# An MLP whose second product is done by Strassen's scheme in one level, after the first product as a whole

## The chip, the core and the metric

The kernel runs on one core of a Trainium2 chip. A core has a matrix engine (TensorE, PE in the profile, with its weight loads listed as PEld), three engines for elementwise work (VectorE = DVE, ScalarE = ACT, GpSimd = POOL), a queue engine that issues transfers (SyncE = SP) and 16 DMA engines. On-chip memory is SBUF, with PSUM for the results of the matrix engine; DRAM lies outside the core. The metric is the device time of one execution in microseconds (us); lower is better. Columns of a tile are its elements along the free axis.

## The reference, cut to what matters

The kernel computes one layer of a streaming encoder: a mixer (latent attention beside a state-space scan) and an MLP. The change touches only the MLP, the last stage:

```python
D_MODEL, D_FF, SEQ, N_META, DEC_SEQ = 1024, 4096, 1024, 16, 32

def hybrid_layer(h, ...):
    ...                                   # attention, scan, gates
    h = h + merged @ p["w_out"]
    a = jax.nn.relu(rmsnorm(h, p["norm_mlp"]) @ p["w_mlp_up"])     # 1024 -> 4096
    h = h + (a * a) @ p["w_mlp_down"]                              # 4096 -> 1024
    return h, ...
```

In the MLP the prompt's 1024 rows and the sample's 32 rows go through together, so that a tile has NQT = 1056 columns, one for each row of h, with D_MODEL or D_FF on the partitions. Everything is f32.

## The kernel before, in words

**Numbers.** To keep f32 accuracy, each operand of a product is split in two parts of type fp32r: hi is a copy of the value in that type (ACT, line 183), lo is the value less hi (DVE or POOL, line 186). A product is three passes into one PSUM sum: hi by hi, hi by lo, lo by hi. `lin_part` issues them: for each block k of 128 contraction rows, for each of the three passes, one matmul for each chunk of columns, `CQ` being three chunks of 352. All its matmuls have one line in the profile, 269; `lin2` gives PSUM tiles of two pools in turn, named acc and pj. Every matmul has a weight load (LDWEIGHTS) of its own.

**Weights.** `Weights` holds the list of all weight units in the order of their use, and each is loaded into a tile `raw` (one DMA on SP's queue) and split into `wh` (ACT) and `wl` (in the MLP POOL), loaded two units ahead of the use and split one ahead. A unit of the first product is 8 blocks of 128 by 128 (512 KB, 1024 columns when split), one of the second is 4 blocks (256 KB, 512 columns).

**The MLP.** The first product gives D_FF = 4096 hidden rows, as 32 units `up(f)` of 128 rows: 72 matmuls of 352 columns each (8 blocks, 3 passes, 3 chunks). Each chunk is then scaled and cut at zero (DVE, line 1492, reading PSUM), squared (ACT, 1493) and split into `ah` (ACT) and `al` (DVE). Four units make a group, eight groups the whole. `down(q)` takes group q's four `ah`/`al` pairs and adds its part of the second product to the 8 accumulators `yacc[:, m]`, 128 rows of the output by 1056 columns each: 36 matmuls of 352 columns for an m, then three DVE additions (line 1510) from PSUM. So first and second product alternate by groups, and nothing of the hidden rows leaves the chip. The accumulators start as h, loaded from DRAM (`h_d`, line 1482) ahead of the MLP.

**Order and end.** The order on each engine is that in which a scheduler puts the instructions of the program; DMAs of the MLP all stand on SP's one queue. In the last group each finished m is turned by PE (transposes of 128 columns, line 1519, `out_rows`), copied by ACT (1521) and stored (1522); the 32 sample rows go by `ys`, a transpose (1541) and `yos` (1543, 1544). The last m of all is done chunk by chunk (396, 396 and 264 columns), so that the outputs of one chunk lie beside the matmuls of the next.

## Time and profile before

| what | value |
|---|---|
| time, median of 3 runs | 2076.12 us (2072.12 to 2077.6) |
| the profiled execution: its own time | 2074.39 us |
| its span, first to last instruction | 2072.6 us |
| mean granted TensorE clock, as a share of full speed | 0.997 |
| PE busy | 2024.0 us, 12944 matmuls |
| DVE, ACT, POOL busy | 1101.4, 731.0, 594.7 us |
| read from and written to DRAM | 123.95 and 44.41 MB |

The rows are all of one execution, whose time lies 1.8 us above its span. A busy time is a sum over an engine's instructions; matmuls are pipelined, so that their listed durations overlap, and how fast PE goes is read from the starts of successive matmuls or from their number in a stretch. The MLP runs from about 1326 us to the end.

### The profile page before, as it was taken

To read this page: it belongs to the slowest core of one execution; us is meant where nothing else is said; L and a number is where in the kernel's file an instruction comes from. 1 tells how busy PE (TensorE), PEld (TensorE's weight loads), DVE (VectorE), ACT (ScalarE), POOL (GpSimd) and SP (SyncE) were. 2 spreads that over 40 slices of the span, in tenths; PEclk is the share of its full clock that TensorE was granted. 3 is DMA by queue.
4 is the path that set the end of the run, shared out by engine and by line. 5 is a ranking of instruction groups with operands and counts; after the bars stand their busy time and mean duration, and the time that the engine had idled before them with its cause. 6 is when DMAs were issued, how large, how long until landed. Compare 5 with 4: busy or idle time off the path is not lost.

```text
span 2072.6 us, 33999 instructions
## 1 busy us (share of the span) xinstructions
PE 2024.0 (98%) x12944; PEld 1917.2 (93%) x12944; DVE 1101.4 (53%) x3071; ACT 731.0 (35%) x1738; POOL 594.7 (29%) x794
## 2 busy tenths in 40 slices
PE   7999999999999999999998999999999999999999
PEld 6988888899999788888887999999999999999998
DVE  5969776534666688888885544332322223222222
ACT  4213222223332567676755233321221212122222
POOL 0577776621222123121221012112221221212121
PEclk9999999999999999999999999999999999999999
DMA  5334444435443101110113534412111120212113
GB/s 144 116 111 120 138 118 143 134 120 173 133 129 117 52 11 28 17 28 17 26 35 98 195 99 132 165 31 57 36 52 51 36 67 26 61 31 57 41 41 105
DMA packets 255893, 170.57 MB, mean 82 GB/s; under 512 B 63210, under 2 KB 239169, under 8 KB 255730
## 3 DMA queue, kind: packets, MB, share of 16 engines
q1 hardware_dynamic: 255728, 168.40, 27.9%
q8 instruction: 102, 1.67, 0.3%
q14 instruction: 61, 0.50, 0.1%
q10 hardware_dynamic: 2, 0.00, 0.0%
HBM read 123.95 MB, written 44.41 MB: 81 GB/s over the span
## 4 chain that ended last, share of the span: by engine, by line
PE 84%; DVE 10%; DMA 3%; ACT 1%; issue 1%; POOL 0%; SPq 0%; ACTq 0%; DVEq 0%; POOLq 0%
PE acc L269 40%; PE pj L269 22%; PE pj L1050 3%; PE po L1283 3%; PE pj L1115 2%; PE pt L1258 1%; PE sp L678 1%; PE Sp L1201 1%; PE Sp L1193 1%; PE Sp L1194 1%; PE Sp L1196 1%; PE Sp L1195 1%; DVE clt L421 1%; PE sp L622 1%; PE pj L1160 1%
## 5 line engine op out<-in xcount | busy, mean ns | idle before, releaser
L186 POOL TENSOR_TENSOR wl<-raw,wh 128x1024 fp32r<-128x1024 f32 (+1 forms) x148 | 291.3, 1968 | 952.2 <-ACT wh L183 853.9
L183 ACT ACTIVATE wh<-raw 128x1024 fp32r<-128x1024 f32 (+2 forms) x166 | 148.6, 895 | 749.1 <-PE acc L269 351.7
L269 PE MATMUL acc<-xh,wh 128*128 128x264 f32 (+6 forms) x736 | 188.7, 337 | 1.8 <-ACT xh L183 1.8
L269 PE MATMUL acc<-xh,wl 128*128 128x264 f32 (+4 forms) x736 | 181.1, 327 | 0.0
L269 PE MATMUL acc<-xl,wh 128*128 128x264 f32 (+5 forms) x736 | 181.0, 327 | 0.0
L269 PEld LDWEIGHTS acc<-xh,wh 128*128 128x128 f32 (+1 forms) x736 | 127.2, 190 | 14.1 <-issue 7.3
L269 PEld LDWEIGHTS acc<-xl,wh 128*128 128x128 f32 (+1 forms) x736 | 129.7, 190 | 2.1 <-issue 0.7
L269 PEld LDWEIGHTS acc<-xh,wl 128*128 128x128 f32 (+1 forms) x736 | 129.6, 190 | 1.8 <-issue 0.7
L1510 DVE TENSOR_TENSOR yacc<-pj,yacc 128x352 f32<-128x352 f32 x96 | 44.5, 517 | 139.5 <-PE pj L269 139.5
L1510 DVE TENSOR_TENSOR yacc<-acc,yacc 128x352 f32<-128x352 f32 (+1 forms) x96 | 44.5, 518 | 113.0 <-PE acc L269 113.0
L186 DVE TENSOR_TENSOR al<-t,ah 128x352 fp32r<-128x352 f32 x96 | 64.7, 700 | 71.9 <-ACT ah L183 71.9
L269 PE MATMUL acc<-sh,wh 128*128 128x352 f32 x384 | 93.0, 325 | 1.5 <-ACT sh L753 1.5
L269 PE MATMUL acc<-sl,wh 128*128 128x352 f32 x384 | 93.5, 324 | 0.0
L269 PE MATMUL acc<-sh,wl 128*128 128x352 f32 x384 | 93.0, 324 | 0.0
L1492 DVE SCALAR_TENSOR_TENSOR t<-acc,rstd 128x352 f32<-128x352 f32 x48 | 23.5, 517 | 117.8 <-PE acc L269 117.8
L269 PE MATMUL acc<-ah,wl 128*128 128x352 f32 (+1 forms) x384 | 85.2, 324 | 0.0
L269 PE MATMUL pj<-al,wh 128*128 128x352 f32 x384 | 84.6, 324 | 0.0
L269 PE MATMUL pj<-ah,wh 128*128 128x352 f32 x384 | 84.3, 323 | 0.0
L269 PE MATMUL acc<-al,wh 128*128 128x352 f32 (+1 forms) x384 | 84.1, 323 | 0.0
L269 PE MATMUL acc<-ah,wh 128*128 128x352 f32 (+1 forms) x384 | 84.0, 323 | 0.0
L269 PE MATMUL pj<-ah,wl 128*128 128x352 f32 x384 | 84.0, 323 | 0.0
L269 PE MATMUL pj<-ha,wh 128*128 128x352 f32 x360 | 79.1, 324 | 0.0
(470 smaller groups left out, 5319.9 us busy)
## 6 DMA issues: line engine op xcount, KB each, us to landing
raw<-in_w_mlp_up_dram SPq DMA_DIRECT2D x32, 512.0 KB
raw<-in_w_mlp_down_dram SPq DMA_DIRECT2D x64, 256.0 KB
raw<-in_w_in_dram SPq DMA_DIRECT2D x29, 512.0 KB
ud<-gst SPq DMA_DIRECT2D x8, 536.0 KB
U<-ud SPq DMA_DIRECT2D x64, 67.0 KB
yd<-Y SPq DMA_DIRECT2D x64, 66.0 KB
yt<-yd SPq DMA_DIRECT2D x8, 528.0 KB
sd<-gw SPq DMA_DIRECT2D x8, 528.0 KB
```

The costliest lines, as they stand in the source:

```text
L183: nc.scalar.activation(hi, src, AF.Copy)
L186: lo_eng.tensor_tensor(lo, src, hi.bitcast(F32), ALU.subtract)
L269: nc.tensor.matmul(pt[:M, :n], lhsT=w[:, k, :], rhs=x(k, c0, n), start=(k == 0 and p == 0), stop=(k == kt - 1 and p == 2),)
L421: eng.tensor_tensor(t1, ar, br, ALU.mult)
L622: nc.tensor.matmul(px[64 * g2:64 * g2 + 64, KC * q:KC * q + KC], lhsT=W[:, q, g, 64 * g2:64 * g2 + 64], rhs=U[:, 2 * g + g2], start=True, ...
L678: nc.tensor.matmul(py[b][:, c], lhsT=cl[hs, q, pr, 1:9].rearrange("p a b -> p (a b)"), rhs=hb[hs, q, pr], start=False, stop=(q == 1),)
L1050: nc.tensor.matmul(ps[:R], lhsT=x[:, c, k0:k0 + R], rhs=w[:, c, :], start=(c == 0 and q == 0), stop=(c == 1 and q == 2))
L1115: nc.tensor.matmul(ps[:R, :384], lhsT=x[:, c, 128 * i:128 * i + R], rhs=w[:, c, :], start=(c == 0 and q == 0), stop=(c == 2 and q == 2))
L1160: nc.tensor.transpose(pt[:, h, z, :R], qt[:, e, h, z], ident[:R, :R])
L1283: nc.tensor.matmul(po[:, :256], lhsT=w, rhs=x, start=st["first"], stop=(last and q == len(grp) - 1))
L1492: nc.vector.scalar_tensor_tensor(t, ps, 0.0, rstd[:, c], op0=ALU.max, op1=ALU.mult)
L1510: nc.vector.tensor_tensor(yacc[:, m, c], ps, yacc[:, m, c], ALU.add)
```

## The change

The 32 units of the first product now run first, all in one go. A group's hidden rows are four blocks k of 128 by 1056; Strassen's scheme (in Winograd's form) cuts them into halves of blocks (two and two) and halves of columns (528 and 528), makes seven blocks of two by 528 out of the four quarters, four by DVE subtractions and three as they are, and each of the seven is split into hi and lo (`place0` to `place6`, 1.08 MB each: 128 partitions by 2112 values). For the groups 0 to 6 they are stored in DRAM (`bd0_0` to `bd6_6`); the seven of group 7 stay. Then the second product runs over 32 pairs: 8 groups (7 first, then 0 to 6, read back into a ring of 12 places) by 4 pairs of output tiles. For a pair POOL makes four sums of weight quarters (128 by 256 each), ACT and POOL split 1024 and 768 columns of weights, and PE does seven products of 12 matmuls (2 blocks, 3 passes, 2 chunks of 264 columns), 84 in all. DVE adds PSUM to `yacc` seven times (`gather`, 128 by 528). Products lie in PSUM tiles X (two buffers), Y and Z (one buffer each, Y also for the outputs' transposes). Before, the same work was 8 quarter products: 2 x 36 matmuls of 352 columns for two output tiles. The accumulators are loaded after the first product; the code before this stage is moved by a few lines (so 269 is 264 there) and otherwise as it was.

```diff
-    units += ups(0, range(GK))
     for q in range(NG):
-        if q + 1 < NG:
-            units += ups(q + 1, [0])
-        units += [(col(flat("w_mlp_down")[q * 512:(q + 1) * 512], m), GK, 128) for m in range(8)]
-        if q + 1 < NG:
-            units += ups(q + 1, range(1, GK))
+        units += ups(q, range(GK))
...
-        yacc = ml.tile([128, 8, NQT], F32, name="yacc")
-        for m in range(8):
-            nc.sync.dma_start(yacc[:, m], h_d[m])
-        ring = {}
...
-            for c0, n, ps in lin2(wh, wl, rh, rl, 8):
-                c = slice(c0, c0 + n)
-                t = ml.tile([128, 352], F32, tag="t", name="t", bufs=2)[:, :n]
-                nc.vector.scalar_tensor_tensor(t, ps, 0.0, rstd[:, c], op0=ALU.max, op1=ALU.mult)
-                nc.scalar.activation(t, t, AF.Square)
-                split(ah[:, c], al[:, c], t, nc.scalar, nc.vector)
-            ring[f] = (ah, al)
...
-        for f in range(GK):
-            up(f)
-        for q in range(NG):
-            if q + 1 < NG:
-                up((q + 1) * GK)
-            down(q)
-            if q + 1 < NG:
-                for f in range(1, GK):
-                    up((q + 1) * GK + f)
...
+    HN = NQT // 2
+    HS = HN // 2
+    blk_d = [dscr(f"bd{q}_", 7, (128, 4 * HN)) for q in range(NG - 1)]
...
+    place = [ml.tile([128, 2, 2, HN], F32R, name=f"place{i}") for i in range(7)]
...
+        for c0, n, ps in lin2(wh, wl, rh, rl, 8):
+            c = slice(c0, c0 + n)
+            t = mu.tile([128, 352], F32, tag="t", name="t", bufs=2)[:, :n]
+            nc.vector.scalar_tensor_tensor(t, ps, 0.0, rstd[:, c], op0=ALU.max, op1=ALU.mult)
+            nc.scalar.activation(a_[:, e % 2, c], t, AF.Square)
+        def keep(i, x):
+            split(place[i][:, 0], place[i][:, 1], x, nc.scalar, nc.vector)
+            if q < NG - 1:
+                nc.sync.dma_start(blk_d[q][i], flat_blk(place[i]))
+        V = nc.vector
+        b1, b2 = hid[0], hid.get(1)
+        lo_, hi_ = slice(0, HN), slice(HN, NQT)
+        if e == 1:
+            hid["t"] = tA = mu.tile([128, 2, HN], F32, tag="tA", name="tA")
+            keep(0, b1[:, :, lo_])
+            V.tensor_tensor(tA, b1[:, :, hi_], b1[:, :, lo_], ALU.subtract)
+            keep(1, tA)
+        if e == 3:
+            tA = hid["t"]
+            V.tensor_tensor(tA, b2[:, :, hi_], tA, ALU.subtract)
+            keep(2, tA)
+            keep(3, b2[:, :, hi_])
+            keep(4, b2[:, :, lo_])
+            V.tensor_tensor(b1[:, :, hi_], b2[:, :, hi_], b1[:, :, hi_], ALU.subtract)
+            keep(5, b1[:, :, hi_])
+            V.tensor_tensor(b1[:, :, lo_], b2[:, :, lo_], tA, ALU.subtract)
+            keep(6, b1[:, :, lo_])
...
+    order = [NG - 1] + list(range(NG - 1))
+    pairs = [(g, j) for g in range(NG) for j in range(4)]
...
+    def w_sums(n):
+        r1, r2 = raws[2 * (n % 2):2 * (n % 2) + 2]
+        T_ = nc.gpsimd.tensor_tensor
+        T_(B(r1, 2), B(r2, 0), B(r2, 1), ALU.add)
+        T_(B(r1, 3), B(r1, 2), B(r1, 0), ALU.subtract)
+        return lambda: (T_(B(r2, 2), B(r1, 0), B(r2, 0), ALU.subtract), T_(B(r2, 3), B(r1, 1), B(r1, 3), ALU.subtract))
+    def w_split(n, e):
+        (h_, l_), r = whl[2 * (n % 2) + e], raws[2 * (n % 2) + e]
+        c = slice(256 * e, 1024)
+        split(h_[:, c], l_[:, c], r[:, c], nc.scalar, nc.gpsimd)
...
+    OPS = {1: (0, 0, 0), 5: (0, 2, 1), 6: (0, 3, 2), 3: (1, 3, 3), 2: (0, 1, 4), 7: (1, 2, 5), 4: (1, 1, 6)}
+    for f in range(NG * GK):
+        up(f)
+        if f == NG * GK - 2:
...
+    rights.close()
+    banks.close()
...
+    yps = ctx.enter_context(tc.tile_pool(reuse_waits="tile", name="yps", bufs=1, space=PSUM))
+    zps = ctx.enter_context(tc.tile_pool(reuse_waits="tile", name="zps", bufs=1, space=PSUM))
+    xps = ctx.enter_context(tc.tile_pool(reuse_waits="tile", name="xps", bufs=2, space=PSUM))
+    yacc = [md.tile([128, NQT], F32, name=f"yacc{m}") for m in range(8)]
+    for m in range(2):
...
+    place += [md.tile([128, 2, 2, HN], F32R, name=f"place{i}") for i in range(7, 12)]
...
+    def blk_load(x):
+        g, i = divmod(x, 7)
+        if g < NG:
+            nc.sync.dma_start(flat_blk(place[x % 12]), blk_d[order[g]][i])
...
+    def prod(n, p, ps, first, halves=((0, 1),)):
+        g, j = pairs[n]
+        e, wb, i = OPS[p]
+        (h_, l_), x = whl[2 * (n % 2) + e], place[(7 * g + i) % 12]
+        for hs in halves:
+            for k in range(2):
+                for q, (w, u) in enumerate(((h_, 0), (h_, 1), (l_, 0))):
+                    for s in hs:
+                        nc.tensor.matmul(ps[:, s, :HS], lhsT=w[:, 256 * wb + 128 * k:256 * wb + 128 * k + 128],
+                                         rhs=x[:, u, k, HS * s:HS * s + HS],
+                                         start=(first and k == 0 and q == 0), stop=(k == 1 and q == 2), skip_group_check=True)
+        if j == 3:
+            blk_load(7 * g + i + 12)
+    def gather(n, r, c, ps, hs=None):
+        y_ = yacc[2 * pairs[n][1] + r][:, HN * c:HN * c + HN].rearrange("p (s n) -> p s n", s=2)
+        v = ps[:, :, :HS]
+        if hs is not None:
+            y_, v = y_[:, hs:hs + 1], v[:, hs:hs + 1]
+        nc.vector.tensor_tensor(y_, v, y_, ALU.add)
...
+        last = n == N - 1
+        later = w_sums(n + 1) if not last else None
+        X = bank2(xps, "X")
+        prod(n, 1, X, True)
+        gather(n, 0, 0, X)
+        if not last:
+            w_split(n + 1, 0)
+            later()
+        if is_out(n - 1):
+            out_rows(2 * pairs[n - 1][1], 0, 8)
+        Z = bank2(zps, "Z")
+        prod(n, 5, Z, True)
+        gather(n, 1, 1, Z)
+        if n:
+            prod(n - 1, 4, before, False)
+            gather(n - 1, 1, 0, before)
+        if not last:
+            w_split(n + 1, 1)
+            w_load(n + 2)
+        prod(n, 6, X, False)
+        gather(n, 0, 1, X)
+        if is_out(n - 1):
+            out_rows(2 * pairs[n - 1][1] + 1, 0, 8)
+        prod(n, 3, Z, False)
+        gather(n, 0, 1, Z)
+        if is_out(n - 1):
+            out_sample(n - 1)
+        Y = bank2(yps, "Y")
+        prod(n, 2, Y, True)
+        gather(n, 0, 0, Y)
+        prod(n, 7, X, False)
+        gather(n, 1, 1, X)
+        before = X
+    out_rows(6, 0, 8)
+    prod(N - 1, 4, before, False, ((0,), (1,)))
+    for hs in range(2):
+        gather(N - 1, 1, 0, before, hs)
+    out_rows(7, 4, 4)
+    out_rows(7, 0, 4)
+    out_sample(N - 1)
```

Three places show how instructions stand on their engines. The first is VectorE at the border of the two products. Before, there is no such border; this is what stood at the end of a group's first product and the group's second product behind it (`t`, `al`: hidden rows of a unit; `yacc`: accumulators).

```order
L1492 SCALAR_TENSOR_TENSOR t<-pj,rstd 128x352 x2
L186 TENSOR_TENSOR al<-t,ah 128x352 x2
L1492 SCALAR_TENSOR_TENSOR t<-pj,rstd 128x352
L186 TENSOR_TENSOR al<-t,ah 128x352
L1510 TENSOR_TENSOR yacc<-acc,yacc 128x352 x3
L1510 TENSOR_TENSOR yacc<-pj,yacc 128x352 x3
```

Now, from the last unit of the first product on (line 186 is the split's lo, `tA` and `hid0` are sums of hidden rows, `yacc0<-X` is the first gather of the second product):

```order
L1501 SCALAR_TENSOR_TENSOR t_18756<-acc_18677,rstd_13853 128x352
L186 TENSOR_TENSOR place4_15673<-hid1_18586,place4_15673 128x1056
L1519 TENSOR_TENSOR tA_18576<-hid1_18586,tA_18576 128x1056
L1523 TENSOR_TENSOR hid0_18401<-hid1_18586,hid0_18401 128x2x528
L186 TENSOR_TENSOR place3_15672<-hid1_18586,place3_15672 128x1056
L1525 TENSOR_TENSOR hid0_18401<-hid1_18586,tA_18576 128x2x528
L186 TENSOR_TENSOR place2_15671<-tA_18576,place2_15671 128x1056
L186 TENSOR_TENSOR place5_15674<-hid0_18401,place5_15674 128x1056
L186 TENSOR_TENSOR place6_15675<-hid0_18401,place6_15675 128x1056
L1624 TENSOR_TENSOR yacc0_18803<-X_18839,yacc0_18803 128x528
L1624 TENSOR_TENSOR yacc0_18803<-Y_18901,yacc0_18803 128x528
```

Eight instructions of 1056 elements stand between the last unit and the first gather, where three additions of 352 came straight after the unit before. On PE the program's order there is: product 1 into X, product 5 into Z, product 2 into Y, then product 6, which adds to the same X and so stands behind the first gather.

The second place is PE at the end of the program. Before (`pj`, `tp`: PSUM tiles that take transposes):

```order
L269 MATMUL acc<-ah,wh 128x264
L269 MATMUL acc<-al,wh 128x264
L269 MATMUL acc<-ah,wl 128x264
L1541 MATMUL tp<-ident,ys 32x128
L1519 MATMUL pj<-ident,yacc 128x128 x5
L1541 MATMUL tp<-ident,ys 32x128
```

Now (lines 1633 and 1647 are transposes, `place5` with Y is product 2 of the last pair; its products 7 and 4 stand just ahead of these rows):

```order
L1633 MATMUL Y_22222<-ident_63,yacc5_18808 128x128 x8
L1647 MATMUL Y_22248<-ident_63,ys_22247 32x128 x2
L1613 MATMUL Y_22256<-place5_15674,wh_18828 128x264 x4
L1613 MATMUL Y_22256<-place5_15674,wl_18829 128x264 x2
L1613 MATMUL Y_22256<-place5_15674,wh_18828 128x264 x4
L1613 MATMUL Y_22256<-place5_15674,wl_18829 128x264 x2
L1633 MATMUL Y_22283<-ident_63,yacc6_18809 128x128 x8
L1633 MATMUL Y_22309<-ident_63,yacc7_18810 128x128 x4
L1633 MATMUL Y_22317<-ident_63,yacc7_18810 128x128 x4
L1647 MATMUL Y_22326<-ident_63,ys_22325 32x128 x2
```

Every row here that names Y uses the one buffer of that tile, so that each stands behind the copy of the one before; product 2 of the last pair is among them, and 18 transposes follow it where 7 followed the last product before.

The third place is POOL in the steady part of the second product. Before, the splits of the last groups, eight instructions for a group's second product and four for one's first (`raw`, `wh`, `wl`: a weight unit as loaded, its hi and its lo):

```order
L186 TENSOR_TENSOR wl<-raw,wh 128x512 x8
L186 TENSOR_TENSOR wl<-raw,wh 128x1024 x4
L186 TENSOR_TENSOR wl<-raw,wh 128x512 x8
L186 TENSOR_TENSOR wl<-raw,wh 128x1024 x3
L186 TENSOR_TENSOR wl<-raw,wh 128x512 x8
```

Now, for one pair; four pairs take the place of a row of eight instructions:

```order
L186 TENSOR_TENSOR wl<-raw,wh 128x1024
L1553 TENSOR_TENSOR raw<-raw 128x256
L1555 TENSOR_TENSOR raw<-raw 128x256
L1554 TENSOR_TENSOR raw<-raw 128x256
L1555 TENSOR_TENSOR raw<-raw 128x256
L186 TENSOR_TENSOR wl<-raw,wh 128x768
```

A pair's six POOL instructions hold 1792 columns of splits and 1024 of sums, where two output tiles of a group took 1024 columns of splits.

## Rows read from the trace of the kernel before

**Rows 1.** The page: busy time, and the chain that ended last.
```profile
PE 2024.0 (98%) x12944; PEld 1917.2 (93%) x12944; DVE 1101.4 (53%) x3071; ACT 731.0 (35%) x1738; POOL 594.7 (29%) x794
PE 84%; DVE 10%; DMA 3%; ACT 1%; issue 1%; POOL 0%; SPq 0%; ACTq 0%; DVEq 0%; POOLq 0%
```

**Rows 2.** Windows: the MLP stage and two 50 us stretches.
```profile
core 0: us, PE busy (x) PEld busy (x) DVE busy (x) ACT busy (x) POOL busy (x), PEclk, DMA share, GB/s
1326.00:2064.00 738.00, 738.00 (x4631) 737.02 (x4631) 202.14 (x408) 166.02 (x301) 154.86 (x94) 1.00 0.18 53
1450.00:1500.00 50.00, 50.00 (x314) 50.00 (x314) 14.36 (x28) 11.71 (x24) 10.11 (x7) 1.00 0.13 38
1700.00:1750.00 50.00, 50.00 (x314) 50.00 (x313) 13.24 (x23) 13.04 (x25) 9.41 (x6) 1.00 0.13 38
```

**Rows 3.** Timeline of PE: starts (us) of 264-column matmuls, then a transpose.
```profile
2066.51 0.28 PE L269 MATMUL acc<-al,wh 128*128 128x264 f32 x1
2066.63 0.29 PE L269 MATMUL acc<-ah,wl 128*128 128x264 f32 x1
...
2067.37 0.28 PE L269 MATMUL acc<-ah,wl 128*128 128x264 f32 x1
2067.38 0.09 PEld L1541 LDWEIGHTS tp<-ident,ys 128*32 128x32 f32 x1
2067.49 0.27 PE L1541 MATMUL tp<-ident,ys 128*32 128x128 f32 x1
2067.49 0.36 PEld L1519 LDWEIGHTS pj<-ident,yacc 128*128 128x128 f32 x3
2067.60 1.01 PE L1519 MATMUL pj<-ident,yacc 128*128 128x128 f32 x5
```

**Rows 4.** Timeline of PE: starts of 512-column matmuls, elsewhere in the program.
```profile
700.12 0.39 PE L1050 MATMUL pj<-wh,ckh 128*128 128x512 f32 x1
...
701.98 0.39 PE L1050 MATMUL pj<-wh,ckl 128*128 128x512 f32 x1
```

**Rows 5.** Lines of DVE, shapes apart: count, busy us, mean ns of one.
```profile
L1510 DVE TENSOR_TENSOR yacc<-acc,yacc 128x352 f32<-128x352 f32 x93 | 43.0, 518 | 108.8 <-PE acc L269 108.8
L1492 DVE SCALAR_TENSOR_TENSOR t<-acc,rstd 128x352 f32<-128x352 f32 x48 | 23.5, 517 | 117.8 <-PE acc L269 117.8
L186 DVE TENSOR_TENSOR wl<-raw,wh 128x1024 fp32r<-128x1024 f32 x14 | 17.4, 1246 | 0.9 <-ACT wh L183 0.9
L643 DVE TENSOR_TENSOR A<-xs,tb 128x1088 f32<-128x1088 f32 x8 | 14.8, 1846 | 4.0 <-POOL tb L423 3.6 <-ACT xs L630 0.3
L754 DVE SCALAR_TENSOR_TENSOR sl<-st,sh 128x1056 fp32r<-128x1056 f32 x8 | 10.2, 1280 | 23.2 <-ACT sh L753 23.2
```

**Rows 6.** Lines of ACT, shapes apart.
```profile
L183 ACT ACTIVATE wh<-raw 128x1024 fp32r<-128x1024 f32 x97 | 102.7, 1059 | 434.4 <-PE acc L269 223.5 <-PE pj L269 105.0 <-issue 87.3
L1493 ACT ACTIVATE t<-t 128x352 f32<-128x352 f32 x96 | 45.8, 493 | 53.8 <-DVE t L1492 52.8 <-ACT t L1493 0.3
L1521 ACT ACTIVATE yo<-tp 128x512 f32<-128x512 f32 x14 | 8.4, 599 | 28.7 <-PE tp L1519 28.7
L183 ACT ACTIVATE ha<-la 128x1056 fp32r<-128x1056 f32 x6 | 6.2, 1070 | 0.9 <-DMA la<-od 0.9
```

**Rows 7.** Lines of POOL, shapes apart.
```profile
L186 POOL TENSOR_TENSOR wl<-raw,wh 128x1024 fp32r<-128x1024 f32 x83 | 207.1, 2495 | 572.3 <-ACT wh L183 473.9 <-DVE st L1419 79.3 <-ACT ckh L183 9.8
L186 POOL TENSOR_TENSOR wl<-raw,wh 128x512 fp32r<-128x512 f32 x65 | 84.2, 1296 | 380.0 <-ACT wh L183 380.0
L1132 POOL TENSOR_TENSOR rr<-rr,r 128x256 f32<-128x256 f32 x16 | 15.8, 990 | 1.2
L425 POOL TENSOR_TENSOR tt<-tb,ek 128x256 f32<-128x256 f32 x8 | 5.2, 649 | 0.0
```

**Rows 8.** SP's issues, and the DMA view of 1300:1345 (40 slices, 1.125 us each).
```profile
1321.61 4.24 SPq L1482 DMA_DIRECT2D yacc<-hd  x8
GB/s 5 89 144 10 0 0 229 298 174 120 300 74 0 0 0 0 0 97 387 42 170 341 416 413 417 409 424 394 413 417 375 83 171 304 13 0 0 0 0 0
```

**Rows 9.** Timeline of the end, after the last product.
```profile
2065.45 0.57 DVE L1510 TENSOR_TENSOR yacc<-acc,yacc 128x396 f32<-128x396 f32 x1 [2.03 <-PE acc L269]
2067.68 0.43 DVE L1510 TENSOR_TENSOR yacc<-acc,yacc 128x264 f32<-128x264 f32 x1 [1.66 <-PE acc L269]
2068.85 0.28 DVE L1543 COPY yos<-tp 32x128 f32<-32x128 f32 x1 [0.45 <-PE tp L1541]
2069.77 0.44 SPq L1544 DMA_DIRECT2D out_dram<-yos  x1
```

More of the change, by code (lines that the diff above doesn't have):

```diff
@@ L736, in tile_layer @@
                     )
-    pjp = ctx.enter_context(tc.tile_pool(reuse_waits="tile", name="pjp", bufs=3, space=PSUM, side="right"))
+    rights, banks = ctx.enter_context(ExitStack()), ctx.enter_context(ExitStack())
+    pjp = banks.enter_context(tc.tile_pool(reuse_waits="tile", name="pjp", bufs=3, space=PSUM, side="right"))
     with tc.tile_pool(reuse_waits="tile", name="gl", bufs=1) as gl, tc.tile_pool(reuse_waits="tile", name="gls", bufs=1) as gls:
@@ L1388, in tile_layer @@
     st_ = ctx.enter_context(tc.tile_pool(reuse_waits="tile", name="stt", bufs=1))
-    acp = ctx.enter_context(tc.tile_pool(reuse_waits="tile", name="acp", bufs=3, space=PSUM))
+    acp = banks.enter_context(tc.tile_pool(reuse_waits="tile", name="acp", bufs=3, space=PSUM))
     turn = [0]
@@ L1394, in lin2 @@
         return lin(*((acp, "acc") if turn[0] else (pjp, "pj")), *x)
-    tpp = ctx.enter_context(tc.tile_pool(reuse_waits="tile", name="tpp", bufs=2, space=PSUM))
+    tpp = banks.enter_context(tc.tile_pool(reuse_waits="tile", name="tpp", bufs=2, space=PSUM))
     for h in (6, 7):
@@ new lines, in tile_layer, with more_w, more_hl, w_load @@
+    wd = flat("w_mlp_down")
+    order = [NG - 1] + list(range(NG - 1))
+    pairs = [(g, j) for g in range(NG) for j in range(4)]
+    raws, whl = [], []
+    def more_w(pool):
+        for _ in range(2):
+            raws.append(pool.tile([128, 1152], F32, tag="raw", name="raw", bufs=2))
+    def more_hl(pool):
+        whl.append([pool.tile([128, 1152], F32R, tag=t, name=t, bufs=2) for t in ("wh", "wl")])
+    def w_load(n):
+        if n < len(pairs):
+            g, j = pairs[n]
+            for e in range(2):
+                c0 = 256 * j + 128 * e
+                nc.sync.dma_start(raws[2 * (n % 2) + e][:, :512].rearrange("p (k m) -> p k m", k=4),
+                                  wd[512 * order[g]:512 * order[g] + 512, c0:c0 + 128].rearrange("(k p) m -> p k m", p=128))
@@ new lines, in tile_layer @@
+    OPS = {1: (0, 0, 0), 5: (0, 2, 1), 6: (0, 3, 2), 3: (1, 3, 3), 2: (0, 1, 4), 7: (1, 2, 5), 4: (1, 1, 6)}
+    for f in range(NG * GK):
+        up(f)
+        if f == NG * GK - 2:
+            more_w(wp)
+            w_load(0)
+    more_hl(wp)
+    later = w_sums(0)
+    w_split(0, 0)
+    later()
+    more_hl(wp)
+    w_split(0, 1)
+    rights.close()
+    banks.close()
+    md = ctx.enter_context(tc.tile_pool(reuse_waits="tile", name="md", bufs=1))
+    yps = ctx.enter_context(tc.tile_pool(reuse_waits="tile", name="yps", bufs=1, space=PSUM))
@@ new lines, in tile_layer, with bank2 @@
+    for _ in range(2):
+        more_hl(md)
+    def blk_load(x):
+        g, i = divmod(x, 7)
+        if g < NG:
+            nc.sync.dma_start(flat_blk(place[x % 12]), blk_d[order[g]][i])
+    for x in range(7, 12):
+        blk_load(x)
+    def bank2(pool, tag):
+        return pool.tile([128, 2, 512], F32, tag=tag, name=tag)
+    def prod(n, p, ps, first, halves=((0, 1),)):
+        g, j = pairs[n]
+        e, wb, i = OPS[p]
[9 more added lines that the diff above has]
+            blk_load(7 * g + i + 12)
@@ new lines, in gather, with out_rows @@
+    def gather(n, r, c, ps, hs=None):
[4 more added lines that the diff above has]
+        nc.vector.tensor_tensor(y_, v, y_, ALU.add)
+    y_o = o[0].rearrange("b (k t) d -> (b k) t d", t=T)
+    y_s = o[1].rearrange("b l d -> (b l) d")
+    def out_rows(m, t0, nt):
+        pt = bank2(yps, "Y").rearrange("p a (b c) -> p (a b) c", c=128)[:, :nt]
+        yv = yacc[m].rearrange("p (t c) -> p t c", t=T)
+        for t in range(nt):
+            nc.tensor.transpose(pt[:, t], yv[:, t0 + t, 0:128], ident)
+        yo = md.tile([128, 8, 128], F32, tag="yo", name="yo", bufs=2)[:, :nt]
+        nc.scalar.activation(yo, pt, AF.Copy)
+        nc.sync.dma_start(y_o[:, t0:t0 + nt, m * 128:(m + 1) * 128], yo)
@@ new lines, in out_sample @@
+    def out_sample(n):
+        j = pairs[n][1]
+        ys = md.tile([128, 2, 32], F32, tag="ys", name="ys")
+        pt = bank2(yps, "Y")
+        for e in range(2):
+            nc.vector.tensor_copy(
+                ys[:, e].rearrange("p (c t) -> p c t", t=T),
+                yacc[2 * j + e].rearrange("p (t c) -> p c t", t=T)[:, 128:132, :],
+            )
+            nc.tensor.transpose(pt[0:32, 0, 128 * e:128 * e + 128], ys[:, e], ident)
+        yos = md.tile([32, 256], F32, tag="yos", name="yos", bufs=2)
+        nc.vector.tensor_copy(yos, pt[0:32, 0, 0:256])
+        nc.sync.dma_start(y_s[:, 256 * j:256 * j + 256], yos)
@@ new lines, in tile_layer @@
+    N = len(pairs)
+    is_out = lambda n: 0 <= n < N and pairs[n][0] == NG - 1
+    before = None
+    for n in range(N):
+        last = n == N - 1
[5 more added lines that the diff above has]
+            w_split(n + 1, 0)
+            later()
+        if is_out(n - 1):
[23 more added lines that the diff above has]
+        before = X
```

69 lines of the change are left out of this document (19 added, 50 removed).

## The prediction

> **What bounds the kernel now.** I read the page first: the matrix engine is busy for 98% of the span and makes up 84% of the chain that ended last [rows 1]. The reader then looks at the windows of the stage that the change touches: from 1326 to 2064 us PE is busy 738 of 738 us at the full granted clock, while DVE, ACT and POOL work 202, 166 and 155 us there and the DMA engines 18% [rows 2]. So this stage is a row of matmuls and nothing else, and its time is their number times the spacing of their starts; other engines matter only where the change makes PE wait for them. Two stretches of 50 us hold 314 matmuls each [rows 2], 50 / 314 = 159.2 ns for one of 352 columns. The first and second products, 32 x 72 and 64 x 36 = 2304 matmuls each, take 366.8 us apiece.
>
> **The matmuls.** The first product keeps its 2304 matmuls of 352 columns. The second becomes 32 x 84 = 2688 of 264 columns. The timeline shows that shape: the starts of eight in a row and of what follows run from 2066.51 to 2067.49 us, 122.5 ns each, and 128-column transposes follow 110 ns apart [rows 3]; 512 columns take (701.98 - 700.12) / 8 = 232.5 ns [rows 4]. A line from 352 to 512 columns gives (232.5 - 159.2) / 160 = 0.458 ns a column and 119 ns for 264. I take 122.5, the shape's own row, with 119 to 124 as bounds (the starts are given to 10 ns). 2688 x 122.5 = 329.3 us, so this term is 329.3 - 366.8 = **-37.5 us** (-46.9 to -33.5). It is less than the eighth of 366.8 (45.9) that the count of columns promises, since a short matmul costs more per column.
>
> The page "TensorE: Matmul & The Clock Gate" of the Trainium skill, section "Back-to-back issue gap", speaks against the change: it puts a sustained stream at about 81 ns for 128 columns and 131 for 512. A line between these is an estimate of 98.7 ns for 264 and 110.2 for 352, by which the new product would take 265 us against 254, 11 us more instead of 37.5 less. The rows of this case, 110, 122.5, 159.2 and 232.5 ns, disagree: most of the price here grows with the columns.
>
> **The first product, all in one go.** A group now takes 4 x 72 x 159.2 ns = 45.8 us of PE. Its DVE work is 12 readings of 0.517 us, 7 lo splits and 4 sums of 1056 elements. Such a split takes 1.25 to 1.28 us, and no row exceeds 1.85 [rows 5]; together 20 us (27 at the upper price). ACT has 12 squares of 0.493, 7 hi splits of 1.07 and 4 weight splits of 1.06, 18 us [rows 6]; POOL 4 x 2.5 = 10 [rows 7]. What could bite is the burst behind a group's last unit: eight DVE instructions, 10 us, in front of the next unit's readings. By my walk it ends 13 us after that unit's matmuls. The next unit fills the other PSUM pool until 11.5 us; its readings then wait some 2 us, and PE needs this pool again only at 22.9. Even at 1.85 us apiece (18 us) the cover holds, so I take nothing; were it gone, eight groups would pay each us of excess.
>
> For the stores, 7.6 MB of blocks and 2 MB of weights per 45.8 us are 210 GB/s; eight loads in a row ran at 410 to 424 GB/s [rows 8]. The weight loads of the next two units stand ahead of a burst's stores on SP's queue. Also nothing.
>
> **The border of the products.** Here the same burst has no cover. On PE product 6 of the first pair adds to the X that the first gather has to read, and that gather is behind the burst on DVE. Let 0 be the end of the last unit: three readings with two buffers between DVE and ACT until 2.1 us, the hi of place4 until 3.2, then eight DVE instructions of 1.25 until 13.2; the gather (128 by 528; on a line through 0.43 us for 264 and 0.57 for 396 [rows 9] it takes 0.71) ends at 13.9. Until then PE has three products, 36 x 0.1225 = 4.4 us: about 9 idle. Next, the second pair's weights are late: their `raw` tiles take the room of hidden tiles that the burst still reads, and on POOL the third pair's lo stands in front of the second's. That I walk to another 1. Last, the fourth pair's weights stand on the queue behind six accumulators and five blocks, 3.2 + 5.4 MB, 20 us at 420 GB/s; about 3 more. Together **+13 us**. Bounds: 8, if the late weights cost nothing and the burst is a little shorter; 18, if DVE takes 1.85 us for each of the eight.
>
> **A pair in the steady part.** PE needs 84 x 0.1225 = 10.3 us. DVE: 7 gathers of 0.71 = 5 us. ACT: 1.06 and about 0.85 of weight split. POOL: four sums of 256 columns, 0.65 to 0.99 each, 2.5 for 1024 columns and, between 1.3 and 2.5 us, about 1.9 for 768 [rows 7]: 7.0 to 8.4 us, near 7 as plain sums resemble the cheaper row. Reading back 7 blocks and 8 weight loads per group is 9.6 MB in 41 us, 234 GB/s, under the shown rate [rows 8]. A gather must end before its PSUM tile is used again; at least one product (12 matmuls, 1.47 us) lies between, double its length. So 0, but 32 pairs make small slips count: up to 6 us (0.2 a pair) as bound.
>
> **The end.** Before, the last product ends at 2067.49 [rows 3], its DVE addition at 2068.11, and the last store is issued at 2069.77 [rows 9]; the span ends at 2072.6, 5.1 us after the product, with 7 transposes (0.8 us) of PE work: 4.3 idle. Now Y passes through six uses in turn: 8 transposes, ACT copy (1024 columns, 1.06), 8 more, copy, the sample's transposes and a DVE copy (0.28), only then product 2, gather, 8 transposes, copy, 4, copy of 512 (0.60 [rows 6]), 4, copy, the sample's, store. Walked with 0.1 to 0.2 us between engines, this takes 16.4 us from the end of product 7; PE work in it is 24 matmuls (2.9) and 36 transposes (4.0), so 9.5 idle: **+5.2 us** (3 to 7). The transposes as such are as many as before (72).
>
> **The sum**, against the profiled execution's 2074.4 us (1.7 under the median): 2074.4 - 37.5 + 13 + 5.2 = 2055.1.
>
> **Rivals.**
> 1. *The fixed costs are hidden* (DVE or ACT run ahead of my walk, stalls of 3 to 5 us in all): 2074.4 - 37.5 + 4 = 2041. For it: the other engines are two thirds idle. Against it: the orders of DVE and PE at the border.
> 2. *The steady part slips* by 0.3 to 0.5 us a pair, through late weights or single Y and Z: 10 to 16 us more, about 2068. Against it: each wait has a cover of one product.
> 3. *Slower: POOL becomes the bound of a pair.* Its 7 us are from rows in which DVE was little used; if its four sums and two splits took over 10.3 us, they would set the pace, each us above costing 32. The gain is gone when the stage loses 19.3 us more, at 10.3 + 19.3 / 32 = 10.9 us a pair; at 11.5 the time is 2055 + 38 = 2093. For it: POOL's rows for one shape spread from 0.65 to 0.99. Against it: even the dear row gives 8.4.
> 4. *Slower: the fixed part of a matmul decides.* With the stalls, the gain ends at (366.8 - 18.2) / 2688 = 129.7 ns a matmul; if a shorter matmul saved only half of what its columns promise, 159.2 x 0.875 = 139.3 ns, the product would take 374.4 us and the whole 2074.4 + 7.6 + 18.2 = 2100. For it: the eight rows are a short stretch, which may not show a limit that builds up. Against it: they stand at 122.5, on the line through longer ones. The section of the Trainium skill named above ("TensorE: Matmul & The Clock Gate", "Back-to-back issue gap") points this way.
>
> **How the numbers follow.** My forecast (2046 to 2064) has a chance of 0.57, rival 1 0.14, rival 2 0.12, rival 3 0.07, rival 4 0.03; 0.07 is for what I have not seen. The low end takes the favourable bounds, 2074.4 - 47 + 8 + 3 = 2038; the high end the others, 2074.4 - 33.5 + 18 + 7 = 2066, and 6 for slips: 2072. A difference under 0.3% (6.2 us) can't be told from none here. Faster: 0.57 + 0.14, two thirds of rival 2 (0.08) and 0.04 of the unseen, 0.83; the same: the rest of rival 2 and of the unseen, 0.07; slower: rivals 3 and 4, 0.10.
>
> **What would show it.** After: 2688 matmuls of 264 columns, 408 in a steady 50 us; the stretch of the first product still at 314 per 50 us; at the border a wait of PE on DVE's gather of X, 8 to 10 us long, and two shorter ones for weights; POOL under 8.4 us a pair; the last store 15 to 17 us after product 7. The prediction is wrong if a 50 us window inside the second product shows PE idle, if the spacing there is over 126 ns, or if the burst stops PE in each group (its price: eight times the stall).

## The result and the profile after

The changed kernel takes 2055.9 us (median of 4 runs, 2053.76 to 2061.78) against 2074.16 for the kernel before on the same chips; the ratio is 0.9918, with a 95% interval of 0.9903 to 0.9934. The forecast was 2055. The profiled execution took 2057.28 us, its span is 2055.5, its mean granted clock 0.991.

The page of the changed kernel, which answers to [rows 1]: PE has 384 matmuls more and 34 us less of busy time; POOL and DVE have more to do.

```profile
PE 1990.2 (97%) x13328; PEld 1882.0 (92%) x13328; DVE 1219.0 (59%) x3092; ACT 765.7 (37%) x1690; POOL 737.9 (36%) x922
```

The windows of the changed kernel, with the columns of [rows 2]: two stretches inside one product each, then the border in steps of 5 us.

```profile
1400.00:1650.00 250.00, 250.00 (x1562) 250.00 (x1561) 105.88 (x125) 92.24 (x126) 53.00 (x22) 1.00 0.55 200
1800.00:2000.00 200.00, 200.00 (x1646) 200.00 (x1646) 96.23 (x138) 37.13 (x39) 138.01 (x120) 1.00 0.62 223
...
1695.00:1700.00 5.00, 0.00 (x0) 0.00 (x0) 5.00 (x4) 2.60 (x3) 4.71 (x4) 0.66 0.51 197
1700.00:1705.00 5.00, 0.70 (x3) 0.73 (x4) 4.90 (x6) 0.09 (x1) 3.29 (x4) 0.50 0.78 224
1705.00:1710.00 5.00, 5.00 (x25) 5.00 (x24) 1.33 (x3) 2.00 (x2) 2.43 (x2) 0.50 0.99 374
1710.00:1715.00 5.00, 5.00 (x42) 5.00 (x42) 1.82 (x3) 1.54 (x2) 5.00 (x4) 0.97 1.04 433
...
1755.00:1760.00 5.00, 2.28 (x13) 2.07 (x12) 0.82 (x2) 2.25 (x3) 5.00 (x8) 0.81 1.01 416
```

In the first product PE never stops, and 1562 matmuls in 250 us are 160.0 ns each, as before (a 50 us window counts also those cut at its edges, so the 159.2 of the prediction is a little short). In the second product 1646 in 200 us are 121.5 ns each, and PE does not stop either. At the border PE stands for most of two windows, and the 25 matmuls of the next one run at a granted clock of 0.50.

What PE waited for, in the MLP of the changed kernel (us in all, times, longest):

```profile
PE X L1613 <- DVE yacc L1624: 10.3, 2, 9.5
PE Y L1647 <- ACT yo L1635: 3.4, 2, 2.2
PE X L1613 <- ACT wh L183: 2.7, 1, 2.7
PE Y L1633 <- ACT yo L1635: 1.9, 2, 1.2
...
PE Y L1613 <- DVE place L186: 0.6, 1, 0.6
PE X L1613 <- POOL wl L186: 0.5, 1, 0.5
```

The first row is the wait for the first gather; wh and wl are late weights; the rows with Y stand at the end, but for the one on place.

Three starts on PE's timeline of the changed kernel give the border's loss: the first matmul of the second product, the first behind the gather, and the 421st.

```profile
1689.38 0.41 PE L1613 MATMUL X<-place,wh 128*128 128x264 f32 x2
...
1704.30 1.22 PE L1613 MATMUL X<-place,wh 128*128 128x264 f32 x4 [9.54 <-DVE yacc L1624]
...
1758.55 1.25 PE L1613 MATMUL X<-place,wh 128*128 128x264 f32 x4 [2.72 <-ACT wh L183]
```

420 matmuls took 69.2 us, where 420 x 0.1215 = 51.0 would do: 18.1 lost, and another 1.4 on the slow matmuls behind 1758, 19.5 in all.

The end of the changed kernel, which answers to [rows 9] (product 7 of the last pair ends at 2036.88, where the transposes begin):

```profile
2036.88 1.04 PE L1633 MATMUL Y<-ident,yacc 128*128 128x128 f32 x8
...
2042.52 0.76 PE L1613 MATMUL Y<-place,wh 128*128 128x264 f32 x4 [0.51 <-DVE yos L1649]
...
2050.91 0.60 ACT L1635 ACTIVATE yo<-Y 128x512 f32<-128x512 f32 x1 [2.26 <-DMA out_dram<-yo]
...
2052.63 0.33 SPq L1650 DMA_DIRECT2D out_dram<-yos  x1
```

Product 2 of the last pair starts only at 2042.52, and ahead of 2050.91 ACT stood 2.26 us, in the end for an output buffer whose store had not landed (ahead of the copy before it stood 0.80, for the transposes alone, so the buffer cost some 1.5). From 2036.88 to the span's end are 18.6 us; with 6.9 us of PE work in them, 11.7 are idle, against 4.3 before.

So the terms are: matmuls 2304 x 160.0 = 368.7 against 2688 x 121.5 = 326.6, -42.1; border +19.5; end 11.7 - 4.3 = +7.4; together -15.2. The whole profiled execution differs by -17.1; the other 2 us lie ahead of the MLP, in code that is the same. To leave that part out, the experiments below give the **MLP's length**: from the start of the first matmul `pj<-ha,wh` after 1300 us to the end of the span, in the one profiled execution of each kernel. These are the starts for the kernel before and the changed one:

```profile
1317.79 0.64 PE L269 MATMUL pj<-ha,wh 128*128 128x352 f32 x3
```

```profile
1315.72 0.64 PE L264 MATMUL pj<-ha,wh 128*128 128x352 f32 x3
```

(So the MLP starts earlier than the "about 1326 us" given for the kernel before.) Its length is 754.8 us before and 739.8 after, -15.0.

### The profile page after: what moved, and what is told of

The parts are those of the page before. It is cut to its first block, busy times and chain, and to the rows that moved or that the text cites. A ratio compares the mean times of both kernels' runs of the same rounds, so it can differ in the third digit from the quotient of the medians.

```text
span 2055.5 us, 35157 instructions
## 1 busy us (share of the span) xinstructions
PE 1990.2 (97%) x13328; PEld 1882.0 (92%) x13328; DVE 1219.0 (59%) x3092; ACT 765.7 (37%) x1690; POOL 737.9 (36%) x922
## 4 chain that ended last, share of the span: by engine, by line
PE 81%; DVE 12%; DMA 3%; issue 2%; POOL 1%; ACT 1%; SPq 0%; ACTq 0%; DVEq 0%; POOLq 0%
PE acc L264 32%; PE pj L264 14%; PE X L1613 8%; PE Z L1613 4%; PE pj L1046 3%; PE po L1279 3%; PE pj L1111 3%; PE Y L1613 2%; PE pt L1254 1%; PE sp L673 1%; PE Sp L1197 1%; PE Sp L1189 1%; PE Sp L1190 1%; PE Sp L1192 1%; PE Sp L1191 1%
## 5 line engine op out<-in xcount | busy, mean ns | idle before, releaser
L186 POOL TENSOR_TENSOR wl<-raw,wh 128x1024 fp32r<-128x1024 f32 (+2 forms) x148 | 343.6, 2324 | 725.3 <-ACT wh L183 626.6
L1613 PE MATMUL X<-place,wh 128*128 128x264 f32 x1024 | 168.6, 287 | 13.1 <-DVE yacc L1624 10.3
L1624 DVE TENSOR_TENSOR yacc<-X,yacc 128x528 f32<-128x528 f32 x129 | 90.4, 703 | 117.3 <-PE X L1613 117.1
L1613 PEld LDWEIGHTS X<-place,wh 128*128 128x128 f32 x1024 | 143.5, 190 | 13.8 <-issue 9.7
L1613 PE MATMUL X<-place,wl 128*128 128x264 f32 x512 | 105.1, 286 | 0.5 <-POOL wl L186 0.5
L1613 PE MATMUL Z<-place,wh 128*128 128x264 f32 x512 | 84.5, 287 | 0.0
L1613 PEld LDWEIGHTS X<-place,wl 128*128 128x128 f32 x512 | 80.0, 189 | 0.7 <-POOL wl L186 0.7
L264 PE MATMUL pj<-la,wh 128*128 128x352 f32 x360 | 78.7, 323 | 0.0
L264 PE MATMUL pj<-ha,wl 128*128 128x352 f32 x360 | 78.3, 323 | 0.0
L264 PE MATMUL acc<-la,wh 128*128 128x352 f32 x360 | 77.6, 323 | 0.0
```

What stands on the lines that cost most here:

```text
L186: lo_eng.tensor_tensor(lo, src, hi.bitcast(F32), ALU.subtract)
L264: nc.tensor.matmul(pt[:M, :n], lhsT=w[:, k, :], rhs=x(k, c0, n), start=(k == 0 and p == 0), stop=(k == kt - 1 and p == 2),)
L1613: nc.tensor.matmul(ps[:, s, :HS], lhsT=w[:, 256 * wb + 128 * k:256 * wb + 128 * k + 128], rhs=x[:, u, k, HS * s:HS * s + HS], start=(first ...
L1624: nc.vector.tensor_tensor(y_, v, y_, ALU.add)
```

## Experiments

| kernel | edit of the changed kernel | time, us | MLP's length, us |
|---|---|---|---|
| changed kernel | | 2055.9 | 739.8 |
| half_burst | last group's blocks in two halves | 2052.5 | 730.5 |
| weights_first | fourth pair's weights ahead of blocks | 2056.2 | 736.2 |
| tail | outputs at the end in X and Z, four yo | 2056.9 | 736.6 |
| warm | 72 unused matmuls in the border | 2059.4 (one run) | 740.9 |
| plain | no Strassen: eight products | 2091.1 | 772.3 |
| no_trip | no blocks to and from DRAM | 2054.4 (one run) | 736.0 |
| pool_some | POOL 8.8 us a pair | 2066.1 (one run) | 747.3 |
| pool_over | POOL 13.4 us a pair | 2159.3 (one run) | 839.6 |
| all3 | half_burst, weights_first, tail | 2042.1 | 724.3 |
| all4 | all3, last store on another queue | 2045.0 | 724.6 |

The lengths scatter too. The first product takes 373.7 us in eight of these kernels' profiled executions, but 375.2 in those of warm, plain and no_trip, where the granted clock in the first 30 us of the MLP was 0.94. And from the last product 7 on, the same code takes 18.6 us in the changed kernel, half_burst and warm, but 19.4 to 20.2 in weights_first, no_trip, pool_some and pool_over, where the window of 5 us with product 2 of the last pair shows a granted clock of 0.59 to 0.75 (1.00 in the other three). So a difference in length of 1 to 2 us is not the effect of an edit by itself.

**plain: the change without Strassen's scheme.**

```diff
-        if e == 1:
...
-            V.tensor_tensor(b1[:, :, lo_], b2[:, :, lo_], tA, ALU.subtract)
-            keep(6, b1[:, :, lo_])
+        if e % 2 == 1:
+            keep(e - 1, a_[:, :, lo_])
+            keep(e, a_[:, :, hi_])
...
-    def prod(n, p, ps, first, halves=((0, 1),)):
+    def prod(n, r, c, ps):
...
+        for b in range(2):
+            x = place[(4 * g + 2 * b + c) % 12]
```

> Undoes Strassen's scheme and keeps the rest: first product as a whole, its four quarter blocks per group kept in DRAM, then eight quarter products per group and pair (96 matmuls of 264 columns), no sums of hidden rows or of weights, four gathers of a sum of two products each. Theory (the gain is the number of matmuls, given back in part at the border): 12 x 32 matmuls more at 121 ns, 46.4 us, less most of the border's 19.5 us as only two lo splits stand before the first gather: 2085 to 2095, slower than the kernel before. Rival (the gain comes from the first product as a whole or the shape of 264 columns): 2065 or less.

It took 2091.1 us, ratio to the kernel before 1.0087 (1.0071 to 1.0104). One window of plain, and what its PE waited for in the MLP:

```profile
1800.00:1850.00 50.00, 50.00 (x415) 50.00 (x414) 12.03 (x17) 5.71 (x9) 11.64 (x9) 1.00 0.37 130
```

```profile
PE Y L1614 <- ACT yo L1616: 3.1, 3, 1.2
PE Y L1628 <- ACT yo L1616: 2.5, 2, 1.3
PE Y L1614 <- DVE yacc L1605: 1.6, 2, 0.8
PE Y L1594 <- DVE yos L1630: 0.5, 1, 0.5
```

No row names the border: with two lo splits in place of the burst it costs nothing, and only the end's waits are left. The spacing is the same as with Strassen's scheme, so 384 matmuls more cost 46.7 us (384 x 121.5 ns); less the border's 19.5, with some 4 us more at the end (24 of its matmuls ran at a granted clock of 0.50) and the 1.5 us of the first product, that is the 32.5 us by which its MLP is longer. The gain comes from the number of matmuls alone: beside the kernel before, plain's MLP is 17.5 us longer, of which 264 columns in place of 352 are 4.5 (3072 x 121.5 ns against 368.7 us) and the rest lies mostly in its end.

**half_burst: the burst.**

```diff
-        if e == 3:
+        if q == NG - 1 and e >= 2:
+            tA, k = hid["t"], slice(e - 2, e - 1)
...
+            V.tensor_tensor(tA[:, k], b2[:, k, hi_], tA[:, k], ALU.subtract)
+            keep1(4, b2[:, k, lo_])
+            keep1(2, tA[:, k])
...
+            keep1(6, b1[:, k, lo_])
+        elif e == 3:
```

> For the last group alone the blocks place2 to place6 are made in two halves, one behind the third hidden unit and one behind the fourth, so that eight DVE instructions of 528 elements stand ahead of the first gather in place of eight of 1056. Theory (the first gather waits behind the burst): PE's wait of 9.5 us at the border falls to 4 to 5 us, the stretch at the lower granted clock behind it gets shorter, and the kernel gains 5 to 7 us on 2055.9. Rival (the gather waits for something else, the accumulator's load or the first pair's weights): the wait stays at 9 us and the time at 2056.

The median is 2052.5 (2050.66 to 2054.07; ratio to the kernel before on the same chips 0.9885, 0.9866 to 0.9904), 3.4 less, under the 5 to 7 expected; the MLP's length falls by 9.3 (the profiled execution had 6 us more ahead of the MLP). The waits of half_burst, answering to those of the changed kernel:

```profile
PE X L1627 <- DVE yacc L1638: 6.0, 2, 5.2
...
PE X L1627 <- POOL wl L186: 1.0, 1, 1.0
```

The first gather's wait falls from 9.5 to 5.2 us, as the theory wanted, so the burst is its cause. The stretch at the lower granted clock behind it is hardly shorter: 22 matmuls in 4.85 us of the window 1705 to 1710, which shows 0.50 as before. The wait for wh is gone too (why was not followed up), while one for wl stays.

**weights_first: the queue.**

```diff
-    for x in range(7, 12):
-        blk_load(x)
...
+        if n == 1:
+            for x in range(7, 12):
+                nc.scalar.activation(place[x][:1, 0, 0, 0:1], raws[2][:1, 0:1], AF.Copy)
+                blk_load(x)
```

> The loads of place7 to place11 are made to wait until the weights of the fourth pair have landed, so that on the queue those 5.4 MB stand behind these weights. Theory (the weights of the fourth pair are late because of the place loads ahead of them): PE's wait of 2.7 us some 66 us into the second product goes, with the 1.4 us of lower clock behind it, 2052. Rival (the split on ACT or POOL is late by itself, from the pairs before): the wait stays over 2 us, 2056.

The median says nothing (2056.2, where the theory had 2052); the MLP is 3.6 us shorter, and its end alone 1.2 longer, at the lower granted clock. First the rows of the changed kernel on which the theory rests, SP's issues and POOL's weight sums ahead of the fourth and the sixth pair:

```profile
1706.14 3.13 SPq L1597 DMA_DIRECT2D place<-bd  x5
1710.46 26.90 SPq L1545 DMA_DIRECT2D raw<-in_w_mlp_down_dram  x5
```

```profile
1729.73 0.73 POOL L1553 TENSOR_TENSOR raw<-raw 128x256 f32<-128x256 f32 x1 [12.62 <-DMA raw<-in_w_mlp_down_dram]
...
1754.61 0.73 POOL L1553 TENSOR_TENSOR raw<-raw 128x256 f32<-128x256 f32 x1 [10.98 <-DMA raw<-in_w_mlp_down_dram]
```

The weights are issued behind the five blocks, and POOL idles 12.6 us until they land, and 11.0 us once more later. By the count of matmuls (420 before it) the wait of 2.7 us is that of the sixth pair, not the fourth as the expectation has it. In weights_first this is the one kind of wait on X:

```profile
PE X L1610 <- DVE yacc L1621: 10.3, 2, 9.5
```

No wait for wh or wl is left, so the queue's order was the cause of both.

**tail: the single Y.**

```diff
-        yo = md.tile([128, 8, 128], F32, tag="yo", name="yo", bufs=2)[:, :nt]
+        yo = md.tile([128, 8, 128], F32, tag="yo", name="yo", bufs=4)[:, :nt]
...
+        if last:
+            XT = bank2(xps, "X")
+            out_rows(2 * pairs[n - 1][1], 0, 8, XT)
...
-    out_rows(6, 0, 8)
+    out_rows(6, 0, 8, bank2(zps, "Z"))
...
-    out_rows(7, 4, 4)
+    out_rows(7, 4, 4, XT)
...
```

> The outputs of the last two pairs go through PSUM tiles of X and Z that are free by then, so that product 2 of the last pair waits for no copy out of Y; the output tile yo has four buffers in place of two. Theory (the end is long because six uses of the one Y follow each other): from the end of the last pair's product 7 to the end of the kernel 12 to 14 us in place of 18.6, so 2050 to 2051. Rival (the end is set by the stores' issues and landings, one after the other on SP's queue): 17 us or more from product 7 on, 2055.

The end of tail (the first row is again where product 7 has ended):

```profile
2037.73 1.04 PE L1633 MATMUL X<-ident,yacc 128*128 128x128 f32 x8
...
2038.52 0.73 PE L1613 MATMUL Y<-place,wh 128*128 128x264 f32 x4
...
2046.46 1.77 SPq L1636 DMA_DIRECT2D out_dram<-yo  x2
...
2048.32 0.79 SPq L1650 DMA_DIRECT2D out_dram<-yos  x1
```

Product 2 now follows the transposes directly. From 2037.73 to the span's end at 2052.7 are 15.0 us, 3.6 less than in the changed kernel: between theory and rival. The engines are done at 2046.9, but the last issue comes 1.4 us later behind two others, and the end 4.4 us after that. What the tiles and what the four buffers give by themselves was not tried. The median, 2056.9, does not show the gain.

**all4: who issues the last store.** all3 is the three edits together; all4 gives the last store to ACT's queue.

```diff
-        nc.sync.dma_start(y_s[:, 256 * j:256 * j + 256], yos)
+        (nc.scalar if n == N - 1 else nc.sync).dma_start(y_s[:, 256 * j:256 * j + 256], yos)
```

> The three edits half_burst, weights_first and tail together. Theory (three separate waits): the border's loss falls from 19.5 us to 8 to 10, the end from 18.6 us behind the last product 7 to 15, so 2040 to 2046. Rival (they hide one another, since PE that comes earlier to a wait only waits longer there): 2050 to 2053, no better than half_burst alone.

> As all3, and the last store of sample rows is issued by ACT's queue in place of SP's, where it stood behind two others. Theory (the last issue is late because SP issues the stores one after the other, 0.8 to 1.1 us each): 1 to 2 us less than all3. Rival (the landing of the stores sets the end, whoever issues them): the same as all3.

all3 took 2042.1 us (2038.63 to 2047.59), ratio 0.9847 (0.9826 to 0.9867), the fastest here with all4 (2045.0, ratio 0.9857, 0.9841 to 0.9873); their intervals overlap. PE's longest wait in the MLP of all3 is the first gather's; the other two, at the end, are 0.7 and 0.6 us:

```profile
PE X L1624 <- DVE yacc L1635: 4.6, 1, 4.6
...
```

The MLP is 15.5 us shorter than the changed kernel's; the single edits gave 9.3, 3.6 and 3.2, 16.1 in all, so they hardly hide one another. In all4 the issue moves, but from the end of product 7 on it takes 14.9 us where all3 takes 14.8, and the DMA view of all4 from 2030 to 2045 us (40 slices) shows why that brings nothing:

```profile
2039.62 0.35 ACTq L1661 DMA_DIRECT2D out_dram<-yos  x1
```

```profile
DMA  0000000000899990000079999999999899980000
```

From 2037.5 the DMA engines are busy without a break until 2043.5, at 273 GB/s in the mean; the outputs' landing sets the end, as the rival said.

**warm: the clock.**

```diff
...
+        if n == 0:
+            for _ in range(72):
+                nc.tensor.matmul(X1[:, 0, :HS], lhsT=whl[0][0][:, 0:128], rhs=place[0][:, 0, 0, 0:HS],
+                                 start=True, stop=True, skip_group_check=True)
         prod(n, 6, X, False)
```

> 72 matmuls whose result nobody uses are put on PE in the border wait (into the second pair's X, which starts anew afterwards), 8.7 us of work. Theory (the granted clock falls because PE is idle there): the granted clock stays at 1.00 through the border, the first matmuls after it go at 121 ns and not at 220, and the profiled execution gains 2.5 to 3 us on 2057.3. Rival (the clock falls for another reason, such as the change of shape or the transfers at that time): it falls to about 0.5 there all the same.

The window of warm where the changed kernel shows 0.50, one later on, and its PE's waits on X between 1685 and 1800 us:

```profile
1705.00:1710.00 5.00, 3.38 (x28) 3.19 (x27) 3.80 (x5) 1.06 (x1) 2.39 (x3) 1.00 0.72 246
...
1755.00:1765.00 10.00, 7.46 (x49) 7.25 (x48) 2.11 (x3) 3.46 (x4) 8.53 (x10) 0.83 0.82 330
```

```profile
PE X L1613 <- ACT wh L183: 3.7, 2, 2.5
PE X L1613 <- DVE yacc L1624: 2.5, 2, 1.6
PE X L1613 <- POOL wl L186: 1.1, 1, 1.1
```

The theory of the clock holds at the border: with PE at work it stays at 1.00, and the fall there is due to the wait. The gain hardly comes. The MLP is 1.1 us longer, but 1.5 us of that lie in the first product, ahead of the edit; from the start of the second product on warm is 0.5 us shorter, where 2.5 to 3 were expected. Without the slow matmuls PE is sooner at the weights, and waits there, for wh and wl together 4.8 us in place of 3.2, and behind the last of these waits the clock falls all the same.

**no_trip: the traffic.**

```diff
-            if q < NG - 1:
-                nc.sync.dma_start(blk_d[q][i], flat_blk(place[i]))
...
-        if g < NG:
-            nc.sync.dma_start(flat_blk(place[x % 12]), blk_d[order[g]][i])
+        pass
...
-        (h_, l_), x = whl[2 * (n % 2) + e], place[(7 * g + i) % 12]
+        (h_, l_), x = whl[2 * (n % 2) + e], place[i]
```

> Leaves out the stores of the hidden blocks to DRAM and their loads: every group's second product uses the blocks of the last group, so the numbers are not the reference's, with all instructions of the engines as they were. Theory (the 53 MB each way are hidden, but for the weights that stand behind them at the border): no change of the stretches of the first and second product, 4 to 6 us less at the border, 2051 to 2053. Rival (the traffic slows the engines or the weight loads all along): the matmuls' spacing falls or 10 us and more are gained.

One run, 2054.4, over the 2051 to 2053 expected; the MLP is 3.8 us shorter, and 5.3 from the start of the second product on, where 4 to 6 were expected at the border. A window of each product in no_trip, and its one kind of wait on X:

```profile
1500.00:1550.00 50.00, 50.00 (x314) 50.00 (x313) 19.79 (x23) 16.89 (x23) 9.63 (x4) 1.00 0.18 53
...
1850.00:1900.00 50.00, 50.00 (x412) 50.00 (x412) 24.19 (x35) 9.54 (x10) 34.22 (x30) 1.00 0.18 54
```

```profile
PE X L1610 <- DVE yacc L1621: 9.5, 1, 9.5
```

With 53 and 54 GB/s in place of some 200, PE's pace and DVE's and POOL's busy times are what they were: the traffic is hidden, and what it costs lies at the border: the waits for wh and wl are gone with it, and the second gather's of 0.8.

**pool_some and pool_over: POOL's bound.** Both repeat two of a pair's sums, once and four times.

```diff
         T_(B(r1, 3), B(r1, 2), B(r1, 0), ALU.subtract)
+        for _ in range(4):
+            T_(B(r1, 2), B(r2, 0), B(r2, 1), ALU.add)
+            T_(B(r1, 3), B(r1, 2), B(r1, 0), ALU.subtract)
```

> POOL makes two of a pair's four weight sums twice (same result): 7.3 + 1.5 = 8.8 us of POOL a pair against 10.2 of PE. Theory (POOL is hidden up to PE's time of a pair): the steady part keeps 413 matmuls per 50 us; 1 to 5 us more at the border, where the weights are late already; 2057 to 2063. Rival (POOL is near its bound, by waits between its instructions): 10 us and more.

> POOL makes eight sums more a pair (the same two again and again): 7.3 + 8 x 0.77 = 13.4 us of POOL a pair, above PE's 10.2. Theory (above PE's time of a pair POOL sets the pace): 32 x 3.2 = 104 us more, some 2155 to 2170, slower than before. Rival (weights prepared two pairs ahead, or idle POOL time, absorb it): under 2100.

POOL's rows in the changed kernel, from which these amounts were made (2.40 + 1.85 + 4 x 0.77 = 7.3 us a pair):

```profile
L186 POOL TENSOR_TENSOR wl<-raw,wh 128x1024 fp32r<-128x1024 f32 x32 | 76.9, 2402 | 19.7 <-ACT wh L183 19.7
L186 POOL TENSOR_TENSOR wl<-raw,wh 128x768 fp32r<-128x768 f32 x32 | 59.0, 1847 | 53.0 <-ACT wh L183 53.0
L1555 POOL TENSOR_TENSOR raw<-raw 128x256 f32<-128x256 f32 x62 | 47.4, 768 | 1.1
```

pool_over took 2159.3 us, as expected. POOL is busy 44.0 to 47.0 us of each 50 us between 1700 and 2100, and PE waits for wh eleven times:

```profile
PE X L1616 <- ACT wh L183: 68.9, 11, 12.5
```

pool_some took 2066.1, more than the 2057 to 2063 expected, and 10.2 over the changed kernel; its MLP is 7.5 longer. One of its windows, and POOL ahead of PE's last wait for weights:

```profile
1850.00:1900.00 50.00, 50.00 (x413) 50.00 (x412) 23.88 (x34) 9.44 (x10) 42.59 (x42) 1.00 0.67 242
```

```profile
1800.25 0.75 POOL L1553 TENSOR_TENSOR raw<-raw 128x256 f32<-128x256 f32 x1 [11.97 <-DMA raw<-in_w_mlp_down_dram]
```

From 1850 on PE keeps its pace, so under PE's 10.2 us a pair POOL is hidden. The loss lies ahead of that: PE waits for weights up to 1809, and ahead of the last of these waits POOL itself stood 12.0 us until a weight unit had landed, so it is the loads that are late, longer into the stage than in the changed kernel, and not POOL's speed alone. Another 1.5 us lie in the end, at the lower granted clock. The rival's 10 us and more are met by the total, its cause is not; this is one run.

## Why the prediction was right

**The matmuls.** -37.5 predicted, -42.1 measured, within the bounds: eight rows gave 122.5 ns, a long stretch gives 121.5, and 352 columns cost 160.0 rather than 159.2. plain shows that this term carries the gain. The rule of the Trainium skill's page "TensorE: Matmul & The Clock Gate", section "Back-to-back issue gap", is not borne out for these matmuls: 264 columns cost 121.5 ns and 352 cost 160.0, where a line through its figures gave 98.7 and 110.2, as an estimate.

**The first product.** Nothing lost, as predicted; the burst stays under its cover (no wait of PE there, 160.0 ns a matmul).

**The border.** 13 predicted, 19.5 measured, just over the upper bound of 18. The mechanism was right, and half_burst shows it: PE went on behind the first gather 14.9 us after the last unit, where the walk had the gather end at 13.9, and the two waits up to it are 10.1 us, against 9. The eight DVE instructions took 11.5 us, not 10, since three of them took 1.78 us each beside POOL's weight sums (last section). The second pair's weights were not late. The fourth pair's cost 0.5 us and the sixth pair's, which the walk missed, 2.7, against 3 put down for the fourth; weights_first takes both away. A gather with no product between cost 0.8. The rest is mostly the granted clock, which the prediction did not think of: about 2.8 us on the matmuls behind the first wait and 1.4 behind the last (though in warm, without the first of these, the waits for weights are 1.6 us longer).

**A pair in the steady part.** No slip, as predicted: 84 x 121.5 ns = 10.2 us, and POOL's 7.3 us lie between the 7.0 and 8.4 of the walk. Rival 3 named a real limit: pool_over shows that POOL sets the pace above 10.2 us, and the changed kernel stays 2.9 us under it.

**The end.** +5.2 predicted, +7.4 measured, just over the bound of 7: the chain through Y was walked rightly in its order (16.4 us), and of the 2.2 us more some 1.5 are ACT's wait for an output buffer, of which there are two; the rest is spread over the chain. tail takes 3.6 us back, with the tiles and the buffers changed together.

So -19.3 was predicted for the profiled execution and -17.1 measured, of which -15.0 in the MLP: the matmuls gave 4.6 us more than said, the border and the end took 6.5 and 2.2 more, and 2 us came from ahead of the MLP. Two of the three terms lay over their bounds; that the forecast of 2055 lies within 1 us of the median of 2055.9 is luck, since these errors partly cancel and ahead of the MLP the executions differ by more than that.
